# Five instead of three 64-slot experts in the expert layer of a two-layer encoder

## The chip, the cores and the metric

The kernel runs on one core of one Trainium2 chip. Its metric is the device time of one execution in microseconds (us); a change is judged by the medians of runs on the same chip. A core has TensorE (PE, with its weight loads shown apart as PEld), VectorE (DVE), ScalarE (ACT), GpSimd (POOL) and SyncE (SP), whose queue issues the weight transfers here. Sixteen transfer (DMA) engines carry them from HBM.

## The reference

Two layers of an encoder for 256 tokens of width 1024. Each layer has a mixer (a gated linear recurrence beside latent attention) and a feed-forward part. Layer 0's feed-forward part is dense; layer 1's has eight experts, of which each token uses two:

```python
logits = (t @ w_router).astype(jnp.float32)
top_v, top_i = lax.top_k(logits, TOP_K)              # TOP_K = 2 of 8
top_w = jax.nn.softmax(top_v, axis=-1)
combine = jnp.sum(jax.nn.one_hot(top_i, N_EXPERTS) * top_w[..., None], axis=1)
for e in range(N_EXPERTS):                           # 1024 -> 2816 -> 1024
    out = out + combine[:, e:e + 1] * swiglu(t, w_gate[e], w_up[e], w_down[e])
```

All weights and activations are float32. `setup_inputs()` draws all inputs from seed 0.

## The kernel before

**Program order.** The class `Program` holds a list of weight tiles (items) and of the steps that use them. `load` (line 142) takes the next buffer of a ring and issues one weight transfer on SP's queue (line 148); `split` (line 160) makes two float32r parts of a tile: ScalarE's cast `wh` (line 176) and VectorE's difference `wl` (line 177). Transfers and splits are written a fixed number of items and units ahead of their use; each engine then takes its instructions in the order written, and a transfer into a ring buffer waits until the tile before it there is used up. A step's hooks (`at`, line 1785) put other work, such as the next expert's gather, at a fixed unit of an expert.

**The experts** (`moe`, line 1355). `route` finds both experts of each token. Expert 0 goes first while the other seven are ordered by their token counts (`order_experts`, line 1424); their numbers are read into registers, and from then on the weight addresses follow the order (`of`, line 1466). The string `KINDS` says what each place in the sequence is:

- A big place (`b`) has 128 slots for tokens. Each of its 35 tiles (12 for gate, 12 for up, 11 for down, 1 MB each or 0.75 MB in the last 768 columns) is cut into two units and split, and each product takes three float32r matmuls (`mm3`, line 308). After its split the tile's ring buffer is free.
- A small place (`s`) has 64 slots (`CAP`). Its tiles are not split ("raw"): PE reads the float32 tile itself, with two halves of the columns side by side in the array (`small`, line 1742; lines 1752 and 1775), in eight records per tile. The ring buffer is free when these matmuls are done.

`RANK` (line 61) gives the big places 1 to 7 the first ranks in the order of counts and the small ones the rest. The largest count at a small place must be at most 64, and all others at most 128; else a branch at the end (`overflow`, line 1821) computes the surplus tokens with all weights loaded again.

Experts 1 to 7 use a ring of ten tile buffers. During expert e, the tokens of e + 1 are gathered with one-hot matmuls (`gather`, line 1549), and the result of e - 1 is scattered back (`scatter`, line 1623). At an expert's end `evac_y` (line 1612) takes the result `y` out of PSUM, with ScalarE first; after the last one `evac_gated` does so on VectorE, and `scatter_out` writes the output. `MSCHED` (line 63) says at which units each of these stands, for either kind.

Of the kernel before, what the change touches and what calls it, by code (L numbers as in the profile page):

```python
# [55 lines left out]
START_ORDER = (mybir.EngineType.Activation, mybir.EngineType.DVE, mybir.EngineType.PE)  # L56
ROUTE_ORDER = START_ORDER

KINDS = "bsbbsbbs"
CAP = dict(b=P, s=64)  # L60
RANK = [None] + [sum(KINDS[j] == KINDS[i] for j in range(1, i)) + (0 if KINDS[i] == "b" else KINDS[1:].count("b"))
                 for i in range(1, E)]
# [159 lines left out]
def encoder(ctx: ExitStack, tc, x, c, positions, params, ada_w, ada_b, w_in, w_uq, w_ukv, w_o_mla,  # L222
# [1132 lines left out]
    def moe(l):  # L1355
# [9 lines left out]
        def pm(name):  # L1365
            return B["pp"].tile([P, 512], F32, tag="mm", name=name, bufs=4)
# [54 lines left out]
        NR = E - 1  # L1421
        NBIG = KINDS[1:].count("b")

# [46 lines left out]
        def gu_ap(w, i, k0, nk, c0, n):  # L1470
            return lambda: kview(of(i, w), k0, nk, c0, n)
# [166 lines left out]
        def start(e, i):  # L1638
            nm, small = f"e{e}", KINDS[e] == "s"
            if i == 0:  # L1640
                tag = "big_hi" if e % 2 else "big_lo"
                if small:
                    B["xe", e] = bt(tag, [P, KD, CAP["s"]], F32, f"xe{e}")
                else:
                    xe2 = bt(tag, [P, 2, KD, P], F32R, f"xe{e}")
                    B["xe", e] = (xe2[:, 0], xe2[:, 1])
                B["g"] = pick(e, 0, nm, e == 0, small)
                if e:
                    pick_b(B["g"], nm)
            elif i < 3:  # L1650
                if small:
                    gather(nm, i - 1, None, None, plain=B["xe", e], n=CAP["s"])
                else:
                    gather(nm, i - 1, *B["xe", e])
            else:
                B["back", e] = put_back(B["g"] if e else pick(e, 0, "b0"), e, nm)
# [24 lines left out]
        def gu(e, w, b, key, fn, after):  # L1681
# [3 lines left out]
            def piece(k, *w_):  # L1685
                if k == 0:
                    B[key] = [pm(f"{key}{e}{b}{j}") for j in range(1 if KINDS[e] == "s" else 2)]
                fn(B[key], k, n, *w_)
                if k == KD - 1:
                    after(B[key])  # L1690

            for i in range(4):
                if KINDS[e] == "s":
                    f = lambda raw, i=i: [piece(2 * i + q, raw[:, q, :]) for q in range(2)]
                else:
                    f = lambda q, h_, l_, i=i: piece(2 * i + q, h_[:, 0, :], l_[:, 0, :])
                pr.w(gu_ap(w, e, 2 * i, 2, c0, n), (2, n), "raw" if KINDS[e] == "s" else "k", f, ring="e" if e else "x")

# [229 lines left out]
```

## Time and profile before

| | us |
|---|---|
| median of 3 runs (1451.45 to 1455.13) | 1452.67 |
| the profiled execution | 1453.3 |
| its span | 1451.6 |

| engine | busy, us | share of the span |
|---|---|---|
| PE | 1390.5 | 96% |
| VectorE | 1061.6 | 73% |
| ScalarE | 840.8 | 58% |
| GpSimd | 144.3 | 10% |

The transfers brought 436.59 MB, a mean of 301 GB/s over the span; 276.8 MB of them are expert weights. Busy shares are averages over stages. The expert stage is the second half: expert 0 ends at 825.2 us and the last one at 1441.1 us. In the tables of windows each row is one stretch: its bounds and length, then for PE, PEld, DVE, ACT and POOL the busy time and the number of instructions, then TensorE's granted clock (1.00 is 2.4 GHz, 0.50 is 1.2 GHz), the mean busy share of the transfer engines, and the GB/s that they moved.

### The profile page before, as it was taken

To read this page: it belongs to the slowest core of one execution; us is meant where nothing else is said; L and a number is where in the kernel's file an instruction comes from. 1 tells how busy PE (TensorE), PEld (TensorE's weight loads), DVE (VectorE), ACT (ScalarE), POOL (GpSimd) and SP (SyncE) were. 2 spreads that over 40 slices of the span, in tenths; PEclk is the share of its full clock that TensorE was granted. 3 is DMA by queue.
4 is the path that set the end of the run, shared out by engine and by line. 5 is a ranking of instruction groups with operands and counts; after the bars stand their busy time and mean duration, and the time that the engine had idled before them with its cause. 6 is when DMAs were issued, how large, how long until landed. Compare 5 with 4: busy or idle time off the path is not lost.

```text
span 1451.6 us, 20969 instructions
## 1 busy us (share of the span) xinstructions
PE 1390.5 (96%) x7786; PEld 1058.7 (73%) x7786; DVE 1061.6 (73%) x1460; ACT 840.8 (58%) x1279; POOL 144.3 (10%) x116
## 2 busy tenths in 40 slices
PE   7999999899999899999999999999999999999997
PEld 5977667799988788677877744788784368888732
DVE  4799877799899499877599613898882069988711
ACT  3678854544544498854388513787781167877500
POOL 1021220033232002010021000000000000000000
PEclk8999999999999999999999999999999999999999
DMA  9784667989986254565778999999899999998996
GB/s 320 248 261 131 232 235 240 306 291 320 320 307 220 87 175 158 173 208 204 291 280 312 335 409 414 411 388 397 279 388 378 403 408 400 378 360 312 384 399 268
DMA packets 169134, 436.59 MB, mean 301 GB/s; under 512 B 7336, under 2 KB 63016, under 8 KB 157760
## 3 DMA queue, kind: packets, MB, share of 16 engines
q1 hardware_dynamic: 168400, 434.48, 81.8%
q8 instruction: 63, 1.03, 0.3%
q10 hardware_dynamic: 560, 0.66, 0.1%
q14 instruction: 47, 0.39, 0.1%
q0 software_dynamic: 64, 0.03, 0.0%
HBM read 434.10 MB, written 1.05 MB: 300 GB/s over the span
## 4 chain that ended last, share of the span: by engine, by line
PE 71%; DVE 16%; issue 5%; ACT 4%; DMA 2%; POOL 1%; SPq 0%; DVEq 0%; ACTq 0%; POOLq 0%
DVE wl L177 7%; PE eg L1752 4%; PE dn L310 4%; PE dn L1775 4%; PE dn L311 4%; PE eu L1752 4%; PE dn L309 4%; PE eg L310 3%; PE eg L311 3%; PE eg L309 3%; PE eu L310 3%; PE eu L309 3%; PE eu L311 3%; DVE aacc L394 2%; PE u L309 1%
## 5 line engine op out<-in xcount | busy, mean ns | idle before, releaser
L177 DVE TENSOR_TENSOR wl<-wr,wh 128x1024 fp32r<-128x1024 f32 (+2 forms) x556 | 638.9, 1182 | 86.2 <-ACT wh L176 83.1
L176 ACT CAST wh<-wr 128x1024 fp32r<-128x1024 f32 (+2 forms) x556 | 547.1, 1000 | 207.1 <-PE dn L311 31.7
L1673 DVE TENSOR_TENSOR act<-sg,eu 128x512 f32<-128x512 f32 (+2 forms) x42 | 25.1, 612 | 143.6 <-PE eu L1752 102.5
L310 PE MATMUL eg<-wl,xe 128*128 128x512 f32 x240 | 91.7, 382 | 4.2 <-DVE wl L177 2.9
L310 PE MATMUL eu<-wl,xe 128*128 128x512 f32 x240 | 90.4, 377 | 1.6 <-DVE wl L177 1.6
L311 PE MATMUL eu<-wh,xe 128*128 128x512 f32 x240 | 89.8, 374 | 0.0
L311 PE MATMUL eg<-wh,xe 128*128 128x512 f32 x240 | 89.7, 374 | 0.0
L310 PE MATMUL dn<-wl,ahl 128*128 128x512 f32 x220 | 87.5, 401 | 0.8 <-DVE wl L177 0.8
L311 PE MATMUL dn<-wh,ahl 128*128 128x512 f32 x220 | 85.8, 393 | 0.0
L309 PE MATMUL eg<-wh,xe 128*128 128x512 f32 x240 | 81.0, 379 | 0.0
L309 PE MATMUL eu<-wh,xe 128*128 128x512 f32 x240 | 80.4, 374 | 0.0
L394 DVE SCALAR_TENSOR_TENSOR aacc<-wr,cact,aacc 128x512 f32<-128x512 f32 x84 | 74.9, 895 | 1.1
L309 PE MATMUL dn<-wh,ahl 128*128 128x512 f32 x220 | 75.7, 397 | 0.0
L1752 PE MATMUL eu<-wr,xe 128*64 128x512 f32 (+1 forms) x288 | 66.0, 562 | 0.0
L1752 PE MATMUL eg<-wr,xe 128*64 128x512 f32 (+1 forms) x288 | 65.3, 564 | 0.0
L1664 ACT ACTIVATE sg<-eg 128x512 f32<-128x512 f32 (+2 forms) x42 | 20.6, 534 | 73.2 <-PE eg L1752 73.2
L318 POOL PARTITION_ALL_REDUCE aacc<-aacc x12 | 49.0, 4083 | 132.7 <-DVE aacc L394 67.9
L1775 PE MATMUL dn<-wr,aT 128*64 128x512 f32 x264 | 58.9, 596 | 0.0
L310 PEld LDWEIGHTS eg<-wl,xe 128*128 128x128 f32 x240 | 45.2, 188 | 16.0 <-DVE wl L177 7.2
L310 PE MATMUL g<-wl,hTh 128*128 128x512 f32 x128 | 51.8, 405 | 2.8 <-DVE wl L177 2.8
L310 PEld LDWEIGHTS eu<-wl,xe 128*128 128x128 f32 x240 | 45.1, 188 | 12.3 <-DVE wl L177 3.3
L309 PE MATMUL g<-wh,hTh 128*128 128x512 f32 x128 | 52.8, 418 | 0.0
(422 smaller groups left out, 3205.1 us busy)
## 6 DMA issues: line engine op xcount, KB each, us to landing
wr<-in_moe_w_down_dram SPq DMA_DIRECT2D x88, 1024.0 KB, 7.8
wr<-in_moe_w_gate_dram SPq DMA_DIRECT2D x64, 1024.0 KB, 9.4
wr<-in_moe_w_up_dram SPq DMA_DIRECT2D x64, 1024.0 KB, 7.7
wr<-in_ada_w_dram SPq DMA_DIRECT2D x48, 1024.0 KB, 7.7
wr<-in_w_in_dram SPq DMA_DIRECT2D x30, 1024.0 KB, 5.3
wr<-in_moe_w_gate_dram SPq DMA_DIRECT2D x32, 768.0 KB, 11.0
wr<-in_moe_w_up_dram SPq DMA_DIRECT2D x32, 768.0 KB, 5.7
wr<-in_ffn_w_gate_dram SPq DMA_DIRECT2D x13, 1024.0 KB, 8.0
```

The lines of the kernel that those rows point to most:

```text
L176: i1 = self.nc.scalar.copy(hi, src)
L177: i2 = self.nc.vector.tensor_sub(lo, src, hi.bitcast(F32))
L309: T.matmul(o, lh, rh, start=start, stop=False)
L310: T.matmul(o, lh, rl, start=False, stop=False)
L311: T.matmul(o, ll, rh, start=False, stop=stop)
L318: G.partition_all_reduce(tot, acc, P, bass_isa.ReduceOp.add)
L394: V.scalar_tensor_tensor(acc, raw[:, kk, :], cact[:, k:k + 1], acc, op0=OP.mult, op1=OP.add)
L1664: A.activation(sg[r, cs_], p[r, cs_], AF.Silu)
L1673: V.tensor_mul(act[r, cs_], B["sg"][j][r, cs_], p[r, cs_])
L1752: T.matmul(ps[0][64 * j:64 * j + 64, :sl.stop - sl.start], B["xe", e][:, k, :], raw[:, sl], start=k == 0, stop=k == KD - 1)
L1775: T.matmul(B["dn"][0][64 * m:64 * m + 64, :], a_, raw[:, 512 * m:512 * m + 512], start=f == 0, stop=f == FC - 1)
```

## The change

Places 3 and 6 of the sequence turn from big to small. Of the seven experts ordered by count, the two largest stand at big places (2 and 5), the other five at small ones. `RANK`, the place where the count is compared with 64 (`NBIG`), and the weight forms of the two places follow from the string.

```diff
-KINDS = "bsbbsbbs"
+KINDS = "bsbssbss"
 CAP = dict(b=P, s=64)
 RANK = [None] + [sum(KINDS[j] == KINDS[i] for j in range(1, i)) + (0 if KINDS[i] == "b" else KINDS[1:].count("b"))
                  for i in range(1, E)]
```

## Rows read from the trace of the kernel before

**Rows 1.** The page: the span, and busy time, share and instructions per engine.

```profile
span 1451.6 us, 20969 instructions
...
PE 1390.5 (96%) x7786; PEld 1058.7 (73%) x7786; DVE 1061.6 (73%) x1460; ACT 840.8 (58%) x1279; POOL 144.3 (10%) x116
```

**Rows 2.** Timeline of ScalarE, 1094 to 1099 us: start, length, what, idle before.

```profile
1097.38 1.27 ACT L1616 ACTIVATE ye<-dn,wse 128x512 fp32r<-128x512 f32 x2 [5.39 <-PE dn L311]
```

**Rows 3.** Windows of experts e1 to e7, in this order.

```profile
825.20:897.80 72.60, 72.01 (x365) 28.42 (x365) 12.13 (x20) 13.39 (x26) 0.00 (x0) 1.00 0.99 394
897.80:997.90 100.10, 99.71 (x498) 80.63 (x497) 88.82 (x94) 78.53 (x96) 0.00 (x0) 1.00 1.02 402
997.90:1098.00 100.10, 99.31 (x506) 81.18 (x506) 83.91 (x89) 73.73 (x91) 0.00 (x0) 1.00 0.93 347
1098.00:1172.40 74.40, 72.09 (x363) 27.79 (x360) 12.13 (x20) 13.21 (x27) 0.00 (x0) 1.00 1.00 394
1172.40:1272.80 100.40, 100.00 (x499) 80.90 (x498) 88.84 (x94) 78.61 (x96) 0.00 (x0) 1.00 1.01 395
1272.80:1372.90 100.10, 99.32 (x505) 81.12 (x505) 83.48 (x87) 73.70 (x91) 0.00 (x0) 1.00 0.94 351
1372.90:1441.10 68.20, 65.84 (x300) 23.19 (x296) 10.73 (x14) 4.15 (x10) 0.00 (x0) 1.00 0.93 368
```

**Rows 4.** Waits, 890 to 912 and 1163 to 1185: total us, times, longest.

```profile
ACT wh L176 <- DMA wr<-in_moe_w_gate_dram: 9.9, 3, 8.7
...
PEld eg L309 <- ACT wh L176: 0.8, 1, 0.8
...
ACT wh L176 <- DMA wr<-in_moe_w_gate_dram: 9.6, 3, 7.2
```

**Rows 5.** Waits of SP's queue during e3, 997.9 to 1098.

```profile
SPq L148 <- DVE wl L177: 68.8, 31, 5.5
```

**Rows 6.** Groups during e3 (big): busy us, mean ns, then idle before.

```profile
L177 DVE TENSOR_TENSOR wl<-wr,wh 128x1024 fp32r<-128x1024 f32 (+1 forms) x67 | 74.0, 1153 | 1.5 <-ACT wh L176 1.1
L176 ACT CAST wh<-wr 128x1024 fp32r<-128x1024 f32 (+1 forms) x66 | 65.3, 1001 | 18.1 <-PE eg L311 6.1 <-PE dn L311 5.9 <-PE eu L311 5.2
L310 PE MATMUL eg<-wl,xe 128*128 128x512 f32 (+1 forms) x48 | 18.1, 378 | 0.4 <-DVE wl L177 0.4
...
L1546 PE MATMUL gae<-gbe,xn 128*128 128x64 bf16 x48 | 1.7, 193 | 0.0
```

**Rows 7.** The same groups' view during e4 (small), 1098.0 to 1172.4.

```profile
L1752 PE MATMUL eu<-wr,xe 128*64 128x512 f32 (+1 forms) x96 | 22.4, 564 | 0.0
L1752 PE MATMUL eg<-wr,xe 128*64 128x512 f32 (+1 forms) x96 | 21.9, 565 | 0.0
L1775 PE MATMUL dn<-wr,aT 128*64 128x512 f32 x88 | 19.5, 596 | 0.0
...
L1546 PE MATMUL gae<-gbe,xn 128*128 128x128 bf16 x48 | 3.2, 220 | 0.0
```

**Rows 8.** Timeline of PE in e4: the records of one small tile.

```profile
1103.60 1.94 PE L1752 MATMUL eg<-wr,xe 128*64 128x512 f32 x8
```

**Rows 9.** From 1000 us to the last expert's end: window, and bytes moved.

```profile
1000.00:1441.10 441.10, 434.47 (x2156) 292.45 (x2154) 277.00 (x299) 241.30 (x304) 0.00 (x0) 1.00 0.96 370
...
DMA packets 37931, 163.11 MB, mean 370 GB/s; under 512 B 2655, under 2 KB 2655, under 8 KB 30862
```

**Rows 10.** Windows in which the transfer engines were fully busy.

```profile
840.00:940.00 100.00, 99.02 (x477) 55.12 (x474) 45.23 (x50) 43.84 (x58) 0.00 (x0) 1.00 1.02 411
1120.00:1220.00 100.00, 98.15 (x472) 56.89 (x468) 46.54 (x51) 47.07 (x61) 0.00 (x0) 1.00 1.02 407
1380.00:1420.00 40.00, 38.28 (x181) 13.60 (x180) 5.87 (x7) 2.36 (x4) 0.00 (x0) 1.00 1.01 400
```

**Rows 11.** Two windows of layer 0's dense feed-forward part.

```profile
240.00:260.00 20.00, 20.00 (x97) 16.50 (x96) 15.27 (x19) 9.26 (x11) 1.81 (x4) 1.00 1.09 356
260.00:280.00 20.00, 15.37 (x88) 12.68 (x86) 12.93 (x21) 10.38 (x20) 2.17 (x4) 1.00 1.01 345
```

## The prediction

> **What bounds the kernel now.** Read the page first: TensorE (PE) is busy for 1390.5 of 1451.6 us, so a stage is short where PE has little to do, unless something starves it [rows 1]. The change touches only the expert stage, so the second view is a table of windows, cut where each expert's result leaves PSUM; such an evacuation is one timeline line per expert, of which e3's is shown [rows 2]. Experts e0 to e7 run in that order; e1, e4, e7 are small today, the others big. The table says two things [rows 3]. PE is busy almost throughout in every expert, and a big one takes 100.1 to 100.4 us, a small one 72.6 and 74.4, the last (small, with nothing to prepare) 68.2. But the transfers are hardly idle either: their share is 0.93 to 1.02, at 347 to 402 GB/s. Every expert must bring the same 34.6 MB (1024 x 2816 x 3 weights of 4 bytes), big or small. A small expert eats that in 73 us, 474 GB/s, which no row shows arriving; it lives on what lies in the ring of ten tiles. A big one eats it in 100 us, 346 GB/s, and refills the ring. So the stage alternates between draining and refilling a store of about 10 MB, and the present order (one small after one or two big) just suits that.
>
> Two more views show how close to empty the store comes. After e1 and after e4, both small, ScalarE's first splits of the following big expert wait for their tile: 9.9 us (longest 8.7) and 9.6 us (longest 7.2), while PE waits under 1 us for a split [rows 4]. The store is empty at these two places, and the few split tiles ahead cover it. In the second big expert of a pair it is the reverse: the sync queue (SP) waits 68.8 of 100.1 us for VectorE to give back a tile, and the rate sinks to 347 GB/s [rows 3, 5]. That is the only slack the change can use.
>
> **The change, part by part.** KINDS makes e3 and e6 small; the order becomes b s b s s b s s.
>
> *Work removed.* In e3, by the group rows, 70 splits leave ScalarE (1001 ns) and VectorE (1153 ns, 74.0 us recorded), and 420 PE matmuls in nine groups, the costliest with 18.1 us [rows 6]. *Work added:* the small form, 96 + 96 + 88 records, 22.4 + 21.9 + 19.5 us of PE in e4 [rows 7]. I take the balance from whole experts instead of adding groups, since these durations include the transposes, gathers and scatters: 100.1 - 73.5 (mean of 72.6 and 74.4) = 26.6 us, and twice that 53.2 us less for PE [rows 3].
>
> *Boundaries that the trace doesn't show.* Small after small occurs twice. Below: a gather of 64 columns costs PE 1.7 us against 3.2 for 128 columns [rows 6, 7], so e4's preparation in e3 is, if anything, 1.5 us cheaper than that of a big one. Above: the 5.4 us for which ScalarE stood before a result left PSUM, were PE to stand as well [rows 2]. I take 0: both neighbouring kinds of boundary show PE at work.
>
> *Selection and addresses.* RANK now gives e2 and e5 the two largest counts, and expert ids come from registers as before; 280 weight DMAs of the same sizes in the same queue. No cost, and no cover needed. What moves is when SP may issue: in e3 and e6 it waits for the end of a tile's eight matmul records (1.94 us) [rows 8] instead of the second split's end. Behind a waiting DMA stand only later weight tiles. In e1 and e4 that same wait already rules, and the rate there is 394 [rows 3].
>
> *What is late next: the transfers.* Up to t = 1000 us the new kernel does what the old one did (e3 begins at 997.9). From there to the last expert's end the old kernel moved 163.1 MB in 441.1 us, a mean of 370 GB/s [rows 9]. The new one has to move the same 163.1 MB. Saturated stretches give 411, 407 and 400 GB/s, and the big expert that begins with an empty store, as e5 still will, 395 [rows 3, 10]. The mean of these four is 403. 163.1 / 0.403 = 404.7 us, so the last tile lands at 1404.7. One tile's matmuls behind it, some 2 us [rows 8], give 1406.7 for the end of the last expert against 1441.1: 34.4 us less.
>
> The check from PE's side: without waits it would end at 1441.1 - 53.2 = 1387.9, so about 19 us of waits must appear. By the tile account they lie in e4 (of the 163.1 MB the last four experts are 138.4, so 24.7 of e3 remain at t = 1000; with e4's 34.6 they land by 1000 + 59.3 / 0.403 = 1147.1, the last tile's matmuls end at 1149.1, and PE without waits would be done at 997.9 + 147 = 1144.9: 4 us), at the start of e5 (the next tile lands 2.6 us later, its cast and subtraction take 1.0 and 1.2 [rows 6]: 3 us), and for the rest, 12 us, in e7.
>
> *Prices of a rate.* At 395 the end is 1414.9 (26.2 saved), at 411 it is 1398.8 (42.3 saved). The "DMA: Bandwidth & Descriptors" page of the Trainium skill, section "Where 436 GB/s comes from", says that HBM to SBUF is limited per core to about 358 GB/s; by it the end would be 1000 + 163.1 / 0.358 + 2 = 1457.6, slower than before. This trace disagrees: 411 GB/s for 100 us, with only this core at work [rows 10].
>
> *PE waiting between tiles.* In e4 and e7 PE will stand some tenths of a us to one us before many tiles. I take nothing for the clock: with PE busy 15.37 of 20 us in the dense feed-forward part the granted clock stayed 1.00, the 2.4 GHz level [rows 11]. The upper price is a rival below.
>
> *Sum.* The profiled execution took 1453.3 us, 1.7 over its span of 1451.6; it lies 0.6 above the median of the three runs, 1452.67. 1453.3 - 34.4 = 1418.9; less 0.6, about 1418 us.
>
> **The rivals.**
> 1. Transfers never bind and PE alone decides: 1452.7 - 53.2 = 1399 us. For it: no wait of PE on a DMA of note today [rows 4]. Against it: 474 GB/s for two small experts in a row, where no stretch reaches that. 5 in 100.
> 2. Little or nothing is gained: the transfers don't hold 400 GB/s once the ring never fills, and give the stage's present mean. At 370 nothing changes (1454); at 385 the end is 1425.6, 1437 us for the kernel. For it: even e5, which begins with an empty store, got 395, and e3 and e6, at 347 and 351, pull the mean down [rows 3]. Against it: those two are explained by SP's waits [rows 5]. 10 in 100, half of it beyond 0.3%.
> 3. Slower, through the transfer rate: it falls, with all ten tiles asked for at once, to the 356 GB/s of the stretch at 240 us, where the share is 1.09 and yet the rate is low [rows 11]. 163.1 / 0.356 + 2 = 460.1, end 1460.1, kernel 1472. It decides from 163.1 / 439.1 = 371 GB/s down. Against it: that stretch moves other tiles (narrower rows), and expert tiles held 400 to 411. 3 in 100. The rule of the Trainium skill named above would do the same here.
> 4. The clock falls to the 1.2 GHz level while PE waits for tiles. A tile's 1.94 us become 3.88, 35 tiles 136 instead of 68 us: e4 and e7 some 68 us longer each, so 1418 + 136 less the waits of 19 gives about 1535. Against it: rows 11, and a slow PE no longer waits, which ends the cause. 3 in 100.
> 5. It doesn't do what it says: the third largest of the seven counts exceeds 64 and the overflow branch runs. With the reference's own inputs the counts are 117, 48, 55, 60, 36, 76, 82, 38 for experts 0 to 7; ordered without expert 0: 82, 76, 60. 60 fits, by 4 tokens, and the narrowest gap between second and third logit is 0.012. Price, if it ran: 13 extra passes of 34.6 MB, at 0.403 85.9 us each, over 1100 us. 1 in 100.
>
> **How the numbers follow.** Forecast (transfers bind at 395 to 411 GB/s) 78 in 100, rivals 5, 10, 3, 3, 1. The predicted time is the forecast's, 1418; its own range is 1410 to 1427. The range I give, 1407 to 1435, adds some of rival 2 and the boundaries' few us, and leaves out rival 1, the rest of 2, and 3 to 5. About 0.3%, 4.4 us, is what a measurement of this kernel can tell from no change. Faster: 78 + 5 + 5 = 88; same: 5; slower: 3 + 3 + 1 = 7.
>
> **What would show it.** e3 and e6 as windows of about 73 us with PE busy throughout; e4 about 76 to 79 us; e7 about 78 to 82, with PE waiting for wr tiles by name; from 1000 us to the end a transfer share near 1.00 and about 400 GB/s in every expert, and almost no SP waits on VectorE's subtraction outside e2 and e5. The prediction is wrong if e7 stays at 68 us (PE decides), if the rate with the ring always open is under 390, if PE's clock leaves 1.00, or if weights are loaded beyond 280 tiles.

## The result and the profile after

The changed kernel takes 1417.72 us in the median of four runs (1416.71 to 1421.19), against 1453.08 us before (1451.45 to 1455.13). The ratio is 0.976, with a 95% interval of 0.975 to 0.977, so 35 us are gone; 1418 was forecast.

The page of the profile after, span and engines (before: [rows 1]):

```profile
span 1417.0 us, 19863 instructions
...
PE 1337.8 (94%) x7486; PEld 943.6 (67%) x7486; DVE 895.8 (63%) x1298; ACT 696.1 (49%) x1125; POOL 145.5 (10%) x116
```

PE lost 53 us of busy time, as much as the forecast took out, but the span only 35. The windows of e1 to e7, cut as in [rows 3], then the stretch from 1000 us to the last expert's end, as in [rows 9], show where the rest went. One cut differs: ScalarE did four casts for e5 before it took e4's result, at 1154.2 us, so e4's row ends a microsecond behind its last matmul instead.

```profile
824.00:896.70 72.70, 72.11 (x365) 28.51 (x365) 12.18 (x20) 13.42 (x27) 0.00 (x0) 1.00 0.99 394
896.70:996.40 99.70, 98.92 (x497) 78.98 (x498) 83.48 (x88) 72.95 (x90) 0.00 (x0) 1.00 1.02 403
996.40:1068.10 71.70, 69.38 (x360) 25.59 (x358) 6.98 (x14) 7.52 (x20) 0.00 (x0) 1.00 1.00 396
1068.10:1149.60 81.50, 72.32 (x352) 24.68 (x348) 7.62 (x15) 8.51 (x20) 0.00 (x0) 1.00 1.02 411
1149.60:1254.50 104.90, 103.01 (x506) 81.99 (x508) 87.32 (x91) 77.13 (x94) 0.00 (x0) 0.98 1.02 403
1254.50:1326.20 71.70, 69.38 (x360) 25.58 (x358) 6.59 (x12) 7.52 (x20) 0.00 (x0) 1.00 1.00 397
1326.20:1406.10 79.90, 69.20 (x298) 21.31 (x294) 10.12 (x14) 3.55 (x8) 0.00 (x0) 1.00 0.97 391
1000.00:1406.10 406.10, 379.68 (x1851) 178.19 (x1849) 117.22 (x144) 103.62 (x157) 0.00 (x0) 1.00 1.01 401
```

e3 and e6 fell from 100.1 to 71.7 us each, 56.8 together. e4 gave back 7.1, the big e5 4.5 and e7 11.7, 23.3 together. Cut at the last matmuls, the gain is 57.9 and what was given back 24.4 (8.5, 3.8 and 12.2): the same 33.5 us remain, and the other 1.5 lie ahead of e3. The transfer share is 0.97 or more in every row, where e3, e6 and e7 had 0.93 or 0.94. In e4 PE is busy 72.3 of 81.5 us. The waits of its weight loads, which can stand while PE still works, name what it lacks (total us, times, longest):

```profile
PEld eu L1752 <- DMA wr<-in_moe_w_up_dram: 6.9, 7, 1.5
...
PEld eg L1752 <- DMA wr<-in_moe_w_gate_dram: 6.1, 6, 1.5
```

PE's timeline at the end of e4 shows the rhythm: a tile's eight records, a wait of half a microsecond for the next tile, and then the hole at the start of e5, where PE waits for the first cast:

```profile
1144.11 1.94 PE L1775 MATMUL dn<-wr,aT 128*64 128x512 f32 x8 [0.56 <-DMA wr<-in_moe_w_down_dram]
1146.54 1.94 PE L1775 MATMUL dn<-wr,aT 128*64 128x512 f32 x8 [0.49 <-DMA wr<-in_moe_w_down_dram]
1150.18 0.73 PE L309 MATMUL eg<-wh,xe 128*128 128x512 f32 x2 [1.71 <-ACT wh L176]
```

Before, the chain of waits that ends the last expert ran through PE, which took the last seven tiles without a wait:

```profile
1428.82 12.24 PE L1775 MATMUL dn<-wr,aT 128*64 128x512 f32 x56
```

Now it runs through transfers (start, length, what):

```profile
1327.75 20.34 DMA wr<-in_moe_w_gate_dram
1348.20 20.14 DMA wr<-in_moe_w_down_dram
1368.50 16.15 DMA wr<-in_moe_w_up_dram
1384.77 19.26 DMA wr<-in_moe_w_down_dram
1404.07 1.96 PE dn L1775 x8
```

The tiles of this chain land 16 to 20 us after their issue, and behind the last there is one tile of matmuls, 1.96 us, as the sum had it.

### The profile page after: what moved, and what is told of

It reads as the page before. It is cut to its first block, busy times and chain, and to the rows that moved or that the text cites. A ratio compares the mean times of both kernels' runs of the same rounds, so it can differ in the third digit from the quotient of the medians.

```text
span 1417.0 us, 19863 instructions
## 1 busy us (share of the span) xinstructions
PE 1337.8 (94%) x7486; PEld 943.6 (67%) x7486; DVE 895.8 (63%) x1298; ACT 696.1 (49%) x1125; POOL 145.5 (10%) x116
## 3 DMA queue, kind: packets, MB, share of 16 engines
HBM read 434.10 MB, written 1.05 MB: 307 GB/s over the span
## 4 chain that ended last, share of the span: by engine, by line
PE 60%; DVE 16%; DMA 11%; issue 5%; ACT 4%; POOL 1%; SPq 1%; DVEq 0%; ACTq 0%; POOLq 0%
DVE wl L177 6%; PE eg L1752 5%; PE dn L1775 5%; PE eu L1752 5%; DMA wr<-in_moe_w_up_dram 4%; DMA wr<-in_moe_w_gate_dram 3%; DMA wr<-in_moe_w_down_dram 3%; PE dn L310 3%; PE dn L311 3%; PE dn L309 2%; DVE aacc L394 2%; PE eg L310 2%; PE eg L311 2%; PE eu L310 2%; DMA wr<-in_w_in_dram 2%
## 5 line engine op out<-in xcount | busy, mean ns | idle before, releaser
L177 DVE TENSOR_TENSOR wl<-wr,wh 128x1024 fp32r<-128x1024 f32 (+3 forms) x416 | 485.6, 1196 | 90.1 <-ACT wh L176 87.3
L176 ACT CAST wh<-wr 128x1024 fp32r<-128x1024 f32 (+3 forms) x416 | 408.7, 999 | 180.6 <-DMA wr<-in_moe_w_gate_dram 27.2
L1752 PE MATMUL eu<-wr,xe 128*64 128x512 f32 (+1 forms) x480 | 111.8, 564 | 4.4 <-DMA wr<-in_moe_w_up_dram 4.0
L1752 PE MATMUL eg<-wr,xe 128*64 128x512 f32 (+1 forms) x480 | 110.5, 565 | 2.6 <-DMA wr<-in_moe_w_gate_dram 2.3
L1775 PE MATMUL dn<-wr,aT 128*64 128x512 f32 x440 | 100.6, 598 | 6.4 <-DMA wr<-in_moe_w_down_dram 6.4
L310 PE MATMUL eg<-wl,xe 128*128 128x512 f32 (+1 forms) x144 | 55.9, 389 | 3.9 <-DVE wl L177 3.9
L310 PE MATMUL eu<-wl,xe 128*128 128x512 f32 (+1 forms) x144 | 54.6, 379 | 1.5 <-DVE wl L177 1.5
L311 PE MATMUL eg<-wh,xe 128*128 128x512 f32 (+1 forms) x144 | 54.5, 379 | 0.0
L311 PE MATMUL eu<-wh,xe 128*128 128x512 f32 (+1 forms) x144 | 54.0, 375 | 0.0
L311 PE MATMUL fg<-fTh,wl 128*128 128x256 f32 x176 | 50.4, 286 | 2.2 <-DVE wl L177 2.2
L309 PE MATMUL eg<-wh,xe 128*128 128x512 f32 (+1 forms) x144 | 50.4, 386 | 1.7 <-ACT wh L176 1.7
```

The costliest lines, as they stand in the source:

```text
L176: i1 = self.nc.scalar.copy(hi, src)
L177: i2 = self.nc.vector.tensor_sub(lo, src, hi.bitcast(F32))
L309: T.matmul(o, lh, rh, start=start, stop=False)
L310: T.matmul(o, lh, rl, start=False, stop=False)
L311: T.matmul(o, ll, rh, start=False, stop=stop)
L1752: T.matmul(ps[0][64 * j:64 * j + 64, :sl.stop - sl.start], B["xe", e][:, k, :], raw[:, sl], start=k == 0, stop=k == KD - 1)
```

## The experiments

The theory: once e1 is through, the number of bytes and the rate at which they come set the end, and PE's time only sets how soon the ring is empty. The main rival: PE's time decides, and what is missing from the 53 us is lost at boundaries of small experts or in PE's own issue.

**The alternation undone, the count kept.**

```diff
-KINDS = "bsbssbss"
+KINDS = "bbbsssss"
```

> Five small experts as in the changed kernel (1417.7 us), but all in a row at the end: b b b s s s s s, so the alternation is undone and the count kept. Theory (transfers bind): while e1 and e2 are big the ring is full and the transfer engines stand; then five experts of 34.6 MB less a store of about 10 MB, 163 MB, must come at 403 GB/s after about 1026 us, so the last expert ends near 1436 and the kernel takes 1447 us (1442 to 1452), most of the gain gone. Rival (PE's time alone decides, or the number of small experts): the same work for PE, so 1418 us.

Measured: 1441.86 us, ratio to the kernel before 0.993 (0.991 to 0.995). Two thirds of the gain are gone with the order alone, so neither the count of small experts nor PE's time decides. Windows of e1, e2, e3 and e5 of this kernel:

```profile
826.60:925.90 99.30, 99.30 (x505) 82.63 (x504) 90.36 (x95) 79.91 (x96) 0.00 (x0) 1.00 0.94 345
925.90:1024.00 98.10, 98.10 (x506) 81.15 (x507) 85.27 (x89) 74.42 (x90) 0.00 (x0) 1.00 0.95 354
1024.00:1094.70 70.70, 68.38 (x356) 25.49 (x358) 7.01 (x14) 6.91 (x19) 0.00 (x0) 1.00 1.00 399
...
1175.30:1259.40 84.10, 72.90 (x354) 23.68 (x354) 6.33 (x13) 6.91 (x18) 0.00 (x0) 1.00 1.02 411
```

While both big ones ran, the transfers stood at 345 and 354 GB/s. Then one small expert lived on the ring (70.7 us), and e5 takes 84.1 us, which is 34.6 MB at 411 GB/s. The time came out 5 us below the expectation, which let the last expert end at 1436; its own figures give 1026 + 163 / 0.403 + 2 = 1432.5. The trace has 1429.2, at a mean of 404 GB/s from 1026 us.

**Another alternating order.**

```diff
-KINDS = "bsbssbss"
+KINDS = "bsbsbsss"
```

> The same count in the order b s b s b s s s. Theory (transfers bind, and no place leaves the ring full for long): the store is emptied by e1, refilled by e2, emptied by e3, refilled by e4; then three small ones run at the transfer rate. The bytes decide, so 1418 us, at most 3 more. Rival (each pair of small neighbours costs a wait of its own; here there are two, e5-e6 and e6-e7, and a longer run of small ones): some 10 us more, 1428.

Measured: 1419.79 us, ratio 0.978 (0.976 to 0.980), not to be told from the changed kernel. A longer run of small experts costs nothing by itself, as long as no stretch before it lets the ring stay full.

**Half of the change.**

```diff
-KINDS = "bsbssbss"
+KINDS = "bsbssbbs"
```

> Only e3 is made small (b s b s s b b s), half of the change. Theory: PE saves 26.6 us, e4 gives back about 4 us and the start of e5 about 3 to waiting for tiles; e6 stays big and refills the ring, so e7 has no waits: 1453.1 - 19 = 1434 us (1431 to 1437). Rival (PE alone decides): 1426.5. Rival (a small one behind a small one gains nothing): 1453.

Measured: 1435.14 us, ratio 0.988 (0.985 to 0.991): the account by bytes, and neither rival. Its windows of e4 and e7 show the difference between an emptied and a refilled ring: e4 takes 81.7 us, as in the changed kernel (81.5), and e7, behind the big e6, 68.5 instead of 79.9:

```profile
1069.30:1151.00 81.70, 73.18 (x355) 24.82 (x350) 7.62 (x15) 8.68 (x20) 0.00 (x0) 1.00 1.02 411
...
1355.60:1424.10 68.50, 66.14 (x301) 23.37 (x300) 10.73 (x14) 4.45 (x10) 0.00 (x0) 1.00 0.93 368
```

**All seven small.**

```diff
-KINDS = "bsbssbss"
+KINDS = "bsssssss"
...
-            overflow()
             fx.close()
```

> All seven ordered experts small (b s s s s s s s), without the overflow branch, so the tokens beyond 64 of the two largest experts are left out. Theory (from the second small expert on, bytes decide): the last expert ends where it does in the changed kernel, 1406 us, and the kernel takes 1418 us (1412 to 1420), although PE has 53 us less to do. Rival (PE decides): 1417.7 - 53 = 1365 us.

Measured: 1410.29 us, ratio 0.971 (0.969 to 0.973). PE has two big experts less to do, and 7 us come of it instead of 53. That is the sharpest case against the rival. The 7 us beyond my 1418 say that the forecast's 403 GB/s wasn't the limit: from 1000 us to the end the mean was 405 GB/s against 401 in the changed kernel, and 1.2 MB less was left to bring. Windows of e3 and e4, in which nothing but small experts stands:

```profile
975.50:1059.70 84.20, 72.89 (x355) 23.67 (x354) 6.32 (x13) 6.91 (x18) 0.00 (x0) 1.00 1.02 411
1059.70:1145.00 85.30, 73.00 (x354) 23.67 (x354) 6.33 (x13) 6.91 (x18) 0.00 (x0) 1.00 1.02 411
```

**Half the bytes, PE's work kept.**

```diff
-                    f = lambda raw, i=i: [piece(2 * i + q, raw[:, q, :]) for q in range(2)]
+                    f = lambda raw, i=i: [piece(2 * i + q, raw[:, 0, :]) for q in range(2)]
...
-                pr.w(gu_ap(w, e, 2 * i, 2, c0, n), (2, n), "raw" if KINDS[e] == "s" else "k", f, ring="e" if e else "x")
+                nk_ = 1 if KINDS[e] == "s" else 2
+                pr.w(gu_ap(w, e, 2 * i, nk_, c0, n), (nk_, n), "raw" if KINDS[e] == "s" else "k", f, ring="e" if e else "x")
...
```

The tiles for down are halved in the same way.

> The changed kernel, but each weight tile of the small experts brings only its first half, and the matmuls read that half twice: half the bytes for e1, e3, e4, e6 and e7, the same instructions on PE. It leaves out half of these experts' weights. Theory (the waits in e4, at the start of e5 and in e7 are for bytes): these three windows go back to PE's pace, 81.5 to 71.7, 104.9 to 100.3 and 79.9 to 68.2 us, so 26 us less: 1392 us (1389 to 1396). Rival (the waits are PE's own, at boundaries between small experts or in issue): 1418 us.

Measured: 1373.86 us, ratio 0.945 (0.944 to 0.947). The direction is the theory's, but it is 18 us faster than it said. Windows of e3, e4, e5, e7, cut at the last matmuls:

```profile
995.60:1063.70 68.10, 68.10 (x356) 25.61 (x356) 6.97 (x14) 7.08 (x19) 0.00 (x0) 1.00 0.77 239
1063.70:1132.10 68.40, 68.40 (x355) 25.96 (x352) 12.25 (x19) 12.72 (x25) 0.00 (x0) 1.00 0.82 272
1132.10:1230.30 98.20, 98.20 (x506) 80.24 (x507) 84.17 (x88) 74.37 (x90) 0.00 (x0) 1.00 0.93 352
...
1298.40:1362.70 64.30, 64.23 (x300) 22.64 (x296) 10.28 (x14) 4.18 (x9) 0.00 (x0) 1.00 0.64 205
```

PE is busy without a break, and a small expert takes 68, not 71 us (e3 of the changed kernel, cut the same way, takes 71.2). So even that e3, whose ring is full at its start, holds 3 us that aren't for bytes, 2.3 of them PE's waits. PE's timeline shows where. In the changed kernel the transposes stand right behind the last up matmul and wait for VectorE's product:

```profile
1007.75 5.32 PE L1752 MATMUL eu<-wr,xe 128*64 128x512 f32 x24
1013.93 0.75 PE L1763 MATMUL at<-ident,act 128*128 128x128 f32 x4 [0.86 <-DVE act L1673]
1014.61 5.80 PE L1752 MATMUL eg<-wr,xe 128*64 128x512 f32 x26
```

With half the bytes they stand two gate tiles later, as the code writes them, with no wait:

```profile
1011.76 3.60 PE L1756 MATMUL eg<-wr,xe 128*64 128x512 f32 x16
1015.29 0.75 PE L1767 MATMUL at<-ident,act 128*128 128x128 f32 x4
```

PE's order is not the written one, then: the program's scheduler moves instructions, and it moved them differently in the two programs. So this experiment changed two things: some 26 of its 44 us are the waits for tiles that the expectation named, and the other 18 come with another order on PE, in the big experts too (98.2 us). Two experiments further down take the order up.

**Half of PE's work, the bytes kept.**

```diff
...
-                for j in range(2):
+                for j in range(2 if k % 2 == 0 else 0):
...
+                    if f % 2 == 0:
...
```

The first stands in gate and up of the small places, the second in their down.

> The changed kernel, but the small experts' matmuls for every second 128 rows of the contraction are left out: half of PE's work on their weights, the same bytes. Theory (bytes decide): from 824 us on the transfers are full anyway; of the 242 MB of seven experts some 10.5 have landed, and 231.7 / 0.403 ends at 1399, so at most 7 us less than now: 1411 us (1408 to 1418). Rival (PE decides): 5 x 34 us less, 1250 us.

Measured: 1419.47 us, ratio 0.977 (0.975 to 0.978): no change against the changed kernel, where the rival has 170 us less. Not even the 7 us that I allowed came. Windows of e1, e2, e4, e7:

```profile
827.10:892.10 65.00, 48.27 (x214) 14.81 (x214) 8.41 (x16) 8.70 (x21) 0.00 (x0) 0.89 1.00 401
892.10:998.00 105.90, 102.81 (x508) 81.84 (x506) 87.32 (x91) 77.39 (x93) 0.00 (x0) 0.98 1.02 403
...
1064.00:1149.00 85.00, 57.83 (x216) 14.83 (x214) 7.62 (x15) 8.68 (x20) 0.00 (x0) 0.80 1.02 411
...
1320.40:1405.40 85.00, 54.91 (x160) 11.87 (x160) 9.90 (x13) 4.24 (x9) 0.00 (x0) 0.79 0.97 390
```

By the last matmuls e1 takes 65.1 us instead of the changed kernel's 70.4, and e2 105.9 instead of 101.7; e3 and e6 are 5 us shorter each, e4 and e7 4 us longer. A faster small expert only hands an emptier ring to the next one.

**Six small, beyond the limit of tokens.**

```diff
-KINDS = "bsbssbss"
+KINDS = "bsssbsss"
```

> Six of seven small (b s s s b s s s): the second largest count, 76, is over 64, so the overflow branch runs. It makes 14 passes over an expert's weights (one for each of two big places, two for each of six small). Priced by bytes at 403 GB/s, as in the prediction, 85.9 us each: 1418 + 1203 = 2620 us. Rival (PE's unsplit matmuls with full 128 columns bind there): by the records of 512 columns in two, some 0.85 us for each of 132 products and the same again in gate and up of 256 columns, about 113 us a pass: 1418 + 1580 = 3000 us. If the branch did not run: 1418.

Measured, one run: 3239.45 us. The branch ran. Taking the changed kernel's span for the part before it, (3237.7 - 1417.0) / 14 = 130 us a pass, more than either price. A window of that length in the branch has PE busy 126.6 of 130 us while the transfers have 277 GB/s:

```profile
2000.00:2130.00 130.00, 126.59 (x527) 89.47 (x526) 9.94 (x22) 11.53 (x31) 0.00 (x0) 1.00 0.83 277
```

There PE decides. The rival was nearer, and still 17 us low, since the weights' products cost more than it said: they alone (lines 1847 and 1861) keep PE busy for 123 us of the window, not 113.

```profile
L1847 PE MATMUL og<-ov,xeo 128*128 128x256 f32 x352 | 81.9, 382 | 2.8 <-DMA ov<-in_moe_w_gate_dram 2.8
...
L1861 PE MATMUL dno<-ov,oat 128*128 128x512 f32 x91 | 41.2, 594 | 0.0
```

**One tile more in the ring.**

```diff
-NM = 4
+NM = 5
...
-DC, MC = 1, 2
+DC, MC = 1, 1
```

> The changed kernel with one more tile in the ring of weights (NM 5) and, to make room for it, one pair of split buffers less (MC 1). Theory (bytes decide after 825 us, and the ring is full when e0 ends): one more tile, 1.05 MB, has landed by then, so 1.05 / 0.403 = 2.6 us less: 1415 us. Rival (four pairs of split buffers don't cover the first tiles of a big expert, whose store is empty): the starts of e2 and e5 cost 1.2 us each or more, and the big experts stall on splits: 1418 to 1430 us.

Measured: 1416.39 us, ratio 0.976 (0.974 to 0.978). The median lies 1.3 us below the changed kernel's, which this can't tell from nothing. The rival's 1.2 us and more at the starts of e2 and e5 didn't appear: cut at the last matmuls, e2 and e5 took 101.8 and 104.6 us, against 101.7 and 105.8 in the changed kernel. Nor did the rate rise with one tile more; the window of e4:

```profile
1071.90:1149.30 77.40, 71.91 (x354) 25.28 (x350) 7.62 (x15) 8.69 (x20) 0.00 (x0) 1.00 1.02 411
```

So the ring's depth isn't what holds the transfers at 411 GB/s.

**PE's order kept as written**, in the changed kernel and in the one before.

```diff
-IN_ORDER = (mybir.EngineType.Activation,)
+IN_ORDER = (mybir.EngineType.Activation, mybir.EngineType.PE)
```

> The changed kernel with PE's instructions of the experts kept in the order in which the code writes them, as ScalarE's are already (IN_ORDER). In the changed kernel the transposes of a block stand directly behind the last up matmul and wait 0.6 to 0.9 us for VectorE's product, three times in e3; with half the bytes they stood two tiles later and there was no such gap. Theory (bytes decide): e3 and e6 get some 3 us shorter, but that only empties the ring sooner, e4 and e7 give it back: 1415 us, at most 4 less than now (1413 to 1419). Rival (these gaps add to the time, about 3 us in each of five small experts and 2 in each of two big ones): 1399 us.

Measured: 1417.30 us, ratio 0.976 (0.975 to 0.977). e3's waits are gone:

```profile
996.40:1064.00 67.60, 67.60 (x354) 25.45 (x352) 6.40 (x14) 6.57 (x19) 0.00 (x0) 1.00 1.01 401
1000.00:1403.00 403.00, 374.99 (x1848) 175.16 (x1844) 118.39 (x144) 104.37 (x157) 0.00 (x0) 1.00 1.01 403
```

and the kernel isn't measurably faster. That is the theory's case once more: by the last matmuls e3 and e6 are 3.0 and 3.1 us shorter than in the changed kernel, and e4 and e7 1.7 and 2.9 us longer.

> The same pinning in the kernel before the change, where the ring is full for long and PE decides. Theory: here the gaps count, about 3 us in each of three small experts and 2 in each of e3 and e6: 1453 - 13 = 1440 us (1437 to 1446). Rival (pinning itself does nothing or harms, since the other order was chosen to fill waits): 1453 or more.

Measured: 1451.96 us, ratio 0.9994 (0.9983 to 1.0005): no change, and a miss. By the timeline's last down matmuls the small e4 went from 72.7 to 69.4 us, as expected, but the big experts got 0.7 to 1.3 us longer instead of 2 shorter. The written order suits the small ones and not the big ones.

**Both together.** The two edits above in one kernel.

> The changed kernel with PE's order kept and eleven tiles in the ring (one pair of split buffers less). In its profile the ring of eleven shortened the stretch from the end of e0 to the end of e7 by 7.6 us (574.4 against 582.0), while e0 ended 4.7 us later. Theory (bytes decide; what helps is what keeps the transfers busy while PE is slow): with both, the stretch is 8 to 12 us shorter than in the changed kernel, 1408 us (1405 to 1414). Rival (the stretch's gain is scatter between profiled executions): 1416, as measured with the ring of eleven alone.

Measured: 1415.50 us, ratio 0.974 (0.972 to 0.975). It is the fastest version that leaves nothing out, but its interval touches the changed kernel's (0.975 to 0.977): a gain of some 2 us is possible and not shown, and the expected 8 us didn't come. In its profile the stretch from e0's end to e7's is shorter again (572.9 us against 582.0), but e0 ended 7.9 us later, which nearly undoes it; with the ring of eleven alone it was 4.7. Whether that delay is scatter or comes from the missing pair of split buffers no run tells.

## Why the prediction was right, point by point

- **Transfers become the bound at 163.1 / 0.403.** Right, and shown: half of PE's work leaves the time as it is, the same five small experts in another order lose two thirds of the gain, and two more small experts give 7 us instead of 53. Half the bytes takes 44 us off, though 18 of them come with PE's other order. Measured were 162.8 MB in 406.1 us, 401 GB/s.
- **The rate of 403.** The right number, in part by luck. Transfers that are never held back run at 411, as both rows shown of the experiment with seven small ones have it. The mean of 401 is lower because the ring still fills behind e2 and e5: e3 and e6 begin with a full ring and have 396 and 397. The low member of my mean, e5's 395, happened to stand for this effect, and nothing in the sum says that it enters with a quarter; had I taken 411 throughout, the forecast would have been 1410.
- **PE's 53.2 us.** Busy time fell by 52.7 (1390.5 to 1337.8). But a small expert's pace was mis-sized: the 73.5 us came from windows that held 0.6 and 2.3 us without PE's work and the preparation of a big expert, where e3 took 71.7, and 68.1 with the transposes where the code has them. So rival 1's floor of 1399 was too high; the half-byte kernel, with its other order on PE, takes 1374. It cost the forecast nothing only because that floor is not reached.
- **Where the waits fall.** e4 was put at 77.7 us (from 1071.4 to 1149.1) and took 81.5, since e3 was done earlier; its last matmul ended at 1148.5. e5's hole was put at 3 us: PE stood 1.71 us for the cast and 0.53 for the subtraction. e7 was put at 78 to 82 us and took 79.9. The end was put at 1406.7 and came at 1406.1.
- **Boundaries of small experts at 0.** Right within what the runs can tell: the order with another boundary and a longer run of small ones took 1419.79 us.
- **Rival 2 and the page's limit.** The rate did not sink when the ring was open all the time; it stood at 411. The limit of 358 GB/s on the "DMA: Bandwidth & Descriptors" page of the Trainium skill (section "Where 436 GB/s comes from") is contradicted by these rows, on one core.
- **Rival 4, the clock.** The sign that was named, a clock off 1.00, appeared in small: after the hole at the start of e5 the granted clock fell for a moment, as the window shows (0.57 in the mean, so most of it at the 1.2 GHz level), and e5 as a whole had 0.98:

```profile
1152.00:1156.00 4.00, 4.00 (x12) 3.12 (x11) 3.80 (x5) 4.00 (x5) 0.00 (x0) 0.57 1.02 405
```

  The half microsecond before each tile of e4 and e7 did not lower it; both rows have 1.00. With half of PE's work it fell in earnest, to a mean of 0.79 and 0.80 in e7 and e4, and the last expert still ended at 1405.4: there the waits took the slower PE up. That kernel has half the records, so the price of 1535 us, for all of them at 1.2 GHz, is not tested.
- **Rival 5, the overflow.** 60 tokens fit into 64 slots, and the branch stayed out. Its price of 85.9 us a pass was too low; it is 130, set by PE.

What stays open: a big expert took 98.1 us in the order with three big ones first, and with half the bytes, but 100.1 before [rows 3]. The traces show another order on PE again: at 98.1 us the transposes stand in fours and PE never waits, while e3 of the kernel before has some of them in pairs and two waits of 0.4 us for VectorE's subtraction. That the order is the cause is not shown: the written order has the transposes in fours too, with two waits of 1.0 us, and gave 100.8. What holds the transfers at 411 GB/s is open too.

## What to carry to other kernels

Where one stage makes an engine faster and the bytes stay, add up the bytes from the point where the ring can no longer refill, divide by the rate of the fullest stretch, and take the later of that and the engine's sum. That is the earliest end: from 1000 us on it gives 1410 here, and 1417.7 were measured, with the ring filling again behind e2 and e5. Look at the transfer share in the slow stages: 0.93 at 347 GB/s beside 411 elsewhere showed what there was to win here. Then order fast and slow consumers so that the ring is neither full nor empty for long: the same five small experts were worth 35 us in one order and 10 in another.

## What the runs showed of the hardware that was not expected

- With transfers the bound, SP's own waits change their kind. In e4 its queue waits for landings of earlier tiles, besides PE (total us, times, longest):

```profile
SPq L148 <- DMA wr<-in_moe_w_up_dram: 12.8, 8, 2.0
...
SPq L148 <- DMA wr<-in_moe_w_down_dram: 7.3, 6, 1.9
...
SPq L148 <- DMA wr<-in_moe_w_gate_dram: 3.3, 4, 1.7
```

  With the 16 to 20 us from issue to landing in the chain above, 411 GB/s are 6 to 8 tiles of 1.05 MB on their way, an estimate. So fewer than the ring's ten are in flight at a time; the rate is 411 GB/s all the same.
- A lower clock of TensorE can be free: with half of PE's matmuls left out, at a mean of 0.79 in the last expert and PE busy 54.91 of 85.0 us, that expert ended at 1405.4, against 1406.1 in the changed kernel at 1.00.
